# An SSD layer whose chunks are issued in two parts, with one projection task between them

## The chip, the cores and the metric

The kernel runs on one core of one Trainium2 chip. The metric is the device time of one execution in microseconds (us), as a median over runs. "The profile" is one execution recorded by the hardware profiler. TensorE is PE, its weight loads are PEld, VectorE is DVE, ScalarE is ACT, GpSimd is POOL, and SP issues the DMAs.

## What is computed

One streaming step of a two-layer encoder, for 1024 frames of a new stream and 32 frames of a running one, with D_MODEL = 1024. Each layer is a mixer and a SwiGLU feed-forward network, each after an RMS norm and added to the residual.

```python
def ssd_scan(x, dt, A, Bm, Cm, S0):          # layer 0: 32 heads of 64, in 4 groups, state 128
    ...
    def step(S, inp):
        xc, dtc, Bc, Cc = inp
        cum = jnp.cumsum(dtc * Ag, axis=1)
        seg = cum[:, :, None] - cum[:, None, :]
        decay = jnp.where(mask, jnp.exp(jnp.where(mask, seg, 0.0)), 0.0)
        xdt = xc * dtc[..., None]
        cb = jnp.einsum('btgn,bsgn->btsg', Cc, Bc)
        y = jnp.einsum('btsg,btsgh,bsghp->btghp', cb, decay, xdt)
        y = y + jnp.einsum('btgn,bghpn->btghp', Cc, S) * jnp.exp(cum)[..., None]
        ...
        S = jnp.exp(last)[..., None, None] * S + jnp.einsum('bsgh,bsghp,bsgn->bghpn', w_end, xdt, Bc)
        return S, y
def swiglu(h, w_gate, w_up, w_down):         # hidden 2816
    return (jax.nn.silu(h @ w_gate) * (h @ w_up)) @ w_down
```

Layer 1 has an HGRN2 mixer (`gla_scan`, 8 heads of 128) in place of the SSD mixer, and a final norm follows.

## The kernel before

**Halves.** Time is cut into two halves. Half 0 has 512 columns in one block; half 1 has 544 (512 of the prompt and 32 of the sample) in two blocks of 272. The stages follow one another: SSD layer (to about 873 us of the profile), FFN of layer 0 (to about 1600), HGRN layer, FFN of layer 1. Inside the FFN the two halves also follow one another.

**Products.** Every float32 operand of a projection is split into a high and a low part, so a product has three matmuls for each of its k steps: L282 (high by high), L283 (low activations), L284 (low weights). Activations are `h`, `l` (normed input), `yh`, `yl` (SSD output), `fh`, `fl` (FFN hidden); weights come by DMA into `raw`, ACT rounds them into `wh`, and DVE subtracts to get `wl`. FFN gate and up products (`ffn_unit`) combine blocks first, and their matmuls are L917 to L919.

**SSD.** A unit is a half and a group of 8 heads: eight units, u0 to u3 in half 0 and u4 to u7 in half 1. A unit has 4 chunks of 128 frames (5 in half 1). `ssd_chunk` issues for a chunk: C by B (L479), four transposes of x (L484), of which DVE makes `xdt` and `xw`; ACT and DVE make the decays in `cumB` (loaded by a broadcast DMA); the transpose of B (L499), copied by ACT to `Btok`; the state's part (L506); `Btok` by `xw` (L509), which renews the state; and eight matmuls `xdt` by decays for y (L520). After each chunk the loop issues a share of the unit's `tasks`: output projections of the unit before, z projections of this one, convolution projections of the next. After the last chunk comes `ssd_gate`, with a sum over partitions by a matmul (L299). Where half 1 begins, `ssd_dt` computes the steps `dt`, and L402 transposes them for all chunks.

**FFN.** The hidden units are worked in slabs of two; a slab's hidden columns `fh`, `fl` then go through w_down (`ffn_outs`, L282 to L284), added to the residual `acc`. Each gate or up unit loads two weight halves and builds eight split weights, some from sums such as `s1` = a21 + a22 (DVE, shown as `s<-raw`). The last slab's outputs of a half are mixed with the next half's norm.

**Order.** A scheduler writes one order per engine from the program's order, its buffers and priorities; each engine then runs its own row of instructions in that order, and waits at an instruction whose operand or buffer is not there.

Of the kernel before, what the change touches and what calls it, by code (L numbers as in the profile page):

```python
# [16 lines left out]
P = 128  # L17
# [13 lines left out]
NG = 4  # L31
# [10 lines left out]
TW = 552  # L42
BUFS = {"xn": 16, "x": 12, "ys": 8, "cb": 4, "xd": 2, "ec": 1, "ss": 1, "xr": 2, "n": 4, "w": 3, "s": 5}
WIDTH = {k: 512 if k == "xr" else TW if k in ("x", "w") else LEN[1] for k in BUFS}


@with_exitstack
def trunk_kernel(ctx, tc, x_prompt, x_sample, state_ssd, cache_conv, state_hgrn,
# [22 lines left out]

    def small(s, w=P, dt=F32):
        return sp.tile([P, w], dt, tag="s", bufs=BUFS["s"], name=nm(s))

# [40 lines left out]

    ident = cp.tile([P, P], F32, name="ident")
    make_identity(nc, ident)
    ones = cp.tile([P, P], F32, name="ones")
    V.memset(ones, 1.0)
    epsc = cp.tile([P, 1], F32, name="epsc")  # L120
    V.memset(epsc, EPS)
    lss = cp.tile([P, 13], F32, name="lss")
    epst = lss[:, 12:13]
    mhalf = cp.tile([P, 8], F32, name="mhalf")
    G.memset(mhalf, -0.5)
    cmask = cp.tile([P, P], F32, name="cmask")
# [4 lines left out]
    rmask = cp.tile([P, LEN[1]], F32, name="rmask")  # L131
    V.memset(rmask, 1.0)
# [3 lines left out]
    for i in range(2):  # L136
        t = cp.tile([P, P], F32, name=f"scz{i}")
        V.memset(t, 0.0)
        scz.append(t)


    acc = [[cp.tile([P, LEN[h]], F32, name=f"acc{h}_{m}") for m in range(KD)] for h in range(2)]

    xss = cp.tile([P, 2, 9], F32, name="xss")
    xr = cp.tile([P, 9], F32, name="xr")

# [36 lines left out]

    vc = cp.tile([P, NVC], F32, name="vc")
    cw = cp.tile([P, 96], F32, name="cw")
    cc = cp.tile([P, 72], F32, name="cc")
    dtb = cp.tile([P, 1], F32, name="dtb")
    acol = cp.tile([P, 1], F32, name="acol")
    dcol = cp.tile([P, 16], F32, name="dcol")
    lbt = cp.tile([P, 6, 8], F32, name="lbt")  # L190
    c1, c0, nc1 = lbt[:, 3, :], lbt[:, 4, :], lbt[:, 5, :]
# [68 lines left out]
    def wraw(parts, kt):  # L260
        raw = wp.tile([P, 1024], F32, tag="raw", bufs=3, name=nm("raw"))
        r3 = raw.rearrange("p (k c) -> p k c", k=kt)
        for (lo, hi, src) in parts:
            dma(r3[:, :, lo:hi], src.rearrange("(k p) c -> p k c", p=P))
        return raw

    @lifted("wl")
    def wsplit(raw, kt):
        wh = wp.tile([P, 1024], F32R, tag="ws", bufs=6, name=nm("wh"))
        wl = wp.tile([P, 1024], F32R, tag="ws", bufs=6, name=nm("wl"))  # L270
        act(wh, raw, AF.Copy)
        tt(wl, raw, wh.bitcast(F32), SUB)
        return (wh.rearrange("p (k c) -> p k c", k=kt), wl.rearrange("p (k c) -> p k c", k=kt))

    def product(ps, w, col, x, b0, bn):

        wh, wl = w
        n = len(x)
        for k, (xh, xl) in enumerate(x):
            a, b = wh[:, k, col:col + P], wl[:, k, col:col + P]  # L280
            mh, ml = xh[:, b0:b0 + bn], xl[:, b0:b0 + bn]
            PE.matmul(ps[:, :bn], a, mh, start=(k == 0), stop=False)  # L282
            PE.matmul(ps[:, :bn], a, ml, start=False, stop=False)  # L283
            PE.matmul(ps[:, :bn], b, mh, start=False, stop=(k == n - 1))  # L284
# [18 lines left out]

    XN = ["xn"] * 16
    XN2 = ["x"] * 12 + ["cb"] * 4
# [16 lines left out]
    def norm(h, wc, out, tags, blocks=None, r=None):  # L322

        for (b0, bn) in blocks or ((0, LEN[h]),):
# [17 lines left out]

    carry = cp.tile([P, NCT, 3], F32, name="carry")
    newc = cp.tile([P, 2, 3, NCT], F32, name="newc")
    Sst = [cp.tile([P, 512], F32, tag="st", bufs=NG, name=f"Sst{g}") for g in range(NG)]
    cumd = [dp.tile([32, LEN[h]], F32, name=f"cumd{h}") for h in range(2)]
# [4 lines left out]
    def ssd_dt(h, xn, blocks):  # L351
# [33 lines left out]
        act(pk[96:128, :L], cum[96:128, :L], AF.Exp)  # L385
        lastc = cp.tile([P, 5], F32, name=f"lastc{h}")
        V.tensor_copy(lastc[96:128, :4], pk[96:128, P - 1:H1:P])
# [4 lines left out]
        dma(lastd[h][:, :nch], lastc[96:128, :nch])  # L392
        elast = cp.tile([P, 32, 5], F32, tag="elast", bufs=2, name=f"elast{h}")
        dma(elast[:, :, :nch], lastd[h][:, :nch].unsqueeze(0).to_broadcast([P, 32, nch]))
        return pk, None, elast

    def ssd_cols(h):
        pk, _, elast = dts[h]
        cols = cp.tile([P, 5, P], F32, tag="cols", bufs=1, name=f"cols{h}")
        for c, (o, n, _) in enumerate(CHUNKS[h]):  # L400
# [173 lines left out]
    def ssd_layer(after, w0):  # L574
# [16 lines left out]
        for i, (h, g) in enumerate(units):  # L591
# [56 lines left out]

    Shb = [cp.tile([P, 512], F32, tag="st", bufs=NG, name=f"Sh{i}") for i in range(2)]
    Sh = [Shb[e // 4][:, (e % 4) * P:(e % 4 + 1) * P] for e in range(8)]  # L650
# [136 lines left out]
    def hgrn_layer(after):  # L787
# [4 lines left out]
        for i, (h, e) in enumerate(units):  # L792
# [38 lines left out]

    def x_stat(h, tag):

        keep = T(tag, "rkeep")
        return rstd_of([acc[h][m][:, :LEN[h]] for m in range(KD)], BLK[h], 1.0 / D, LEN[h], keep)

    def norm_pieces(h, wc, out, blocks, r):

        def piece(m, b0, bn):
            xf = T("n", "xf")  # L840
            stt(xf[:, :bn], acc[h][m][:, b0:b0 + bn], vc[:, wc + m:wc + m + 1], r[:, b0:b0 + bn], MUL, MUL)
            if m == len(out):
                out.append((T("xn", "h", F32R), T("xn", "l", F32R)))
            xh, xl = out[m]
# [43 lines left out]
    def unit_weights(src):  # L888
# [9 lines left out]

        s1 = T("xr", "s1")[:, :512].rearrange("p (k c) -> p k c", k=4)
        yield hl(a11)  # L900
# [137 lines left out]

    def ffn_outs(layer, h, s, hid):

        ws = {}

        def piece(m, b0, bn):
# [58 lines left out]
    def mixer_ffn(mixer, layer, wc, nxt):  # L1102
# [16 lines left out]
        due = ffn_half(layer, 1, xn[1], tx[1], 1, lambda: r.append(nxt and x_stat(0, "ss")),  # L1119
                       [2] if nxt else [1, 1])  # L1120
# [111 lines left out]
```

## Time and profile before

| | |
|---|---|
| median of 3 runs | 2942.97 us (2942.57 to 2947.24) |
| the profiled execution | 2942.06 us |
| its span, first to last instruction | 2940.3 us |
| PE busy | 2855.9 us, 97% |
| PEld busy | 2618.4 us, 89% |
| DVE busy | 2205.6 us, 75% |
| ACT busy | 1551.3 us, 53% |
| mean granted clock of PE | 0.994 |

The profiled execution's time is 1.8 us longer than its span. Matmuls are pipelined, so the busy shares of PE overlap its waits a little; what an engine waited for is in the views of waits, and one place is read in a timeline.

### The profile page before, as it was taken

The page shows a single profiled execution, that of the slowest core. Times are in us where ns is not written, and L with a number is a line of the kernel's source. Part 1 is how long each engine was busy: PE and PEld are TensorE (multiplying, and loading weights), DVE is VectorE, ACT ScalarE, POOL GpSimd, SP SyncE. Part 2 cuts the span into 40 slices and gives each one's busy share as a digit, 9 for nine tenths or more (in the row PEclk, how much of TensorE's full clock was granted, in tenths as well). Part 3 has the DMA queues.
Part 4 walks back from the last instruction along what each step waited for, and adds up shares of the span by engine and source line. Part 5 has one row for each costly group of instructions (what it writes and reads, how often), then busy time and mean ns, then how long its engine had stood idle before and what let it go on. Part 6 is the DMA issues. An engine that isn't in the chain of part 4 may idle for free.

```text
span 2940.3 us, 49353 instructions
## 1 busy us (share of the span) xinstructions
PE 2855.9 (97%) x19655; PEld 2618.4 (89%) x19655; DVE 2205.6 (75%) x3879; ACT 1551.3 (53%) x2944; POOL 52.7 (2%) x156
## 2 busy tenths in 40 slices
PE   7999999999999999999999999999999999999998
PEld 6777788989988999899999888899988999999997
DVE  6877787877887987897777555655578977887777
ACT  6745545554643654455544555655554644454445
POOL 0000001000100000000000000000000000000000
PEclk9999999999999999999999999999999999999999
DMA  5443424343333333322333222222222333323332
GB/s 146 123 111 94 108 76 122 106 113 98 109 80 105 98 98 108 108 80 87 101 94 99 79 79 80 69 76 76 78 84 87 108 96 99 111 87 94 94 94 103
DMA packets 401346, 283.42 MB, mean 96 GB/s; under 512 B 28873, under 2 KB 386778, under 8 KB 401114
## 3 DMA queue, kind: packets, MB, share of 16 engines
q1 hardware_dynamic: 401114, 280.25, 32.7%
q8 instruction: 154, 2.52, 0.4%
q14 instruction: 78, 0.64, 0.1%
HBM read 272.39 MB, written 7.82 MB: 95 GB/s over the span
## 4 chain that ended last, share of the span: by engine, by line
PE 75%; DVE 12%; DMA 6%; ACT 5%; issue 2%; SPq 0%; DVEq 0%; POOL 0%; ACTq 0%; POOLq 0%
PE mm L282 16%; PE mm L284 16%; PE mm L283 16%; PE mm L919 3%; PE mm L917 3%; PE mm L918 3%; PE sc L919 3%; PE sc L917 3%; PE sc L918 3%; DMA cumB<-cumd 3%; DMA raw<-in_ffn_w_gate_dram 2%; DVE wh L89 2%; ACT wh L86 1%; PE sc L509 1%; ACT cumB L86 1%
## 5 line engine op out<-in xcount | busy, mean ns | idle before, releaser
L86 ACT ACTIVATE wh<-raw 128x512 fp32r<-128x512 f32 (+1 forms) x688 | 554.2, 817 | 592.4 <-PE mm L283 363.3
L282 PE MATMUL mm<-h,wh 128*128 128x272 f32 (+2 forms) x2064 | 675.0, 328 | 7.9 <-ACT h L86 3.9
L284 PE MATMUL mm<-h,wl 128*128 128x272 f32 (+2 forms) x2064 | 668.5, 324 | 2.7 <-DVE wl L89 2.7
L283 PE MATMUL mm<-l,wh 128*128 128x272 f32 (+2 forms) x2064 | 668.3, 324 | 1.3 <-DVE l L89 0.9
L89 DVE TENSOR_TENSOR wl<-raw,wh 128x1024 fp32r<-128x1024 f32 x308 | 376.0, 1222 | 150.7 <-ACT wh L86 149.3
L282 PEld LDWEIGHTS mm<-h,wh 128*128 128x128 f32 x2064 | 390.0, 189 | 38.1 <-ACT h L86 4.9
L284 PEld LDWEIGHTS mm<-h,wl 128*128 128x128 f32 x2064 | 390.2, 189 | 33.0 <-DVE wl L89 3.9
L283 PEld LDWEIGHTS mm<-l,wh 128*128 128x128 f32 x2064 | 390.4, 189 | 30.9 <-DVE l L89 3.1
L282 PE MATMUL mm<-fh,wh 128*128 128x272 f32 (+1 forms) x1056 | 343.2, 326 | 8.9 <-DVE fxd L89 7.8
L283 PE MATMUL mm<-fl,wh 128*128 128x272 f32 (+1 forms) x1056 | 342.2, 325 | 1.8 <-DVE fl L89 1.8
L89 DVE TENSOR_TENSOR acc<-mm,acc 128x272 f32<-128x272 f32 (+1 forms) x512 | 259.6, 524 | 110.3 <-PE mm L284 107.6
L284 PE MATMUL mm<-fh,wl 128*128 128x272 f32 (+1 forms) x1056 | 341.1, 324 | 0.6 <-DVE wl L89 0.6
L89 DVE TENSOR_TENSOR wh<-raw,wh 128x512 fp32r<-128x512 f32 x380 | 258.2, 688 | 20.6 <-ACT wh L86 17.7
L917 PE MATMUL mm<-th,wh 128*128 128x272 f32 (+1 forms) x912 | 260.9, 286 | 0.4 <-ACT s L86 0.4
L919 PE MATMUL mm<-th,wh 128*128 128x272 f32 (+1 forms) x912 | 259.6, 285 | 0.2 <-DVE wh L89 0.2
L918 PE MATMUL mm<-tl,wh 128*128 128x272 f32 (+1 forms) x912 | 259.6, 285 | 0.0
L282 PEld LDWEIGHTS mm<-fh,wh 128*128 128x128 f32 x1056 | 198.8, 189 | 26.9 <-DVE fxd L89 9.3
L283 PEld LDWEIGHTS mm<-fl,wh 128*128 128x128 f32 x1056 | 199.6, 189 | 17.7 <-DVE fl L89 3.4
L284 PEld LDWEIGHTS mm<-fh,wl 128*128 128x128 f32 x1056 | 199.5, 189 | 16.1 <-DVE wl L89 1.0
L917 PE MATMUL sc<-h,wh 128*128 128x272 f32 (+1 forms) x608 | 173.7, 286 | 0.5 <-ACT wh L86 0.5
L917 PEld LDWEIGHTS mm<-th,wh 128*128 128x128 f32 x912 | 171.7, 188 | 2.5 <-ACT s L86 1.7
L919 PE MATMUL sc<-h,wh 128*128 128x272 f32 (+1 forms) x608 | 173.3, 285 | 0.0
(261 smaller groups left out, 5961.0 us busy)
## 6 DMA issues: line engine op xcount, KB each, us to landing
raw<-in_ffn_w_down_dram SPq DMA_DIRECT2D x90, 512.0 KB, 3.5
raw<-in_ffn_w_gate_dram SPq DMA_DIRECT2D x88, 512.0 KB, 4.9
raw<-in_ffn_w_up_dram SPq DMA_DIRECT2D x88, 512.0 KB, 3.8
raw<-in_ssd_in_w_dram SPq DMA_DIRECT2D x80, 512.0 KB, 4.6
raw<-in_hgrn_in_w_dram SPq DMA_DIRECT2D x64, 512.0 KB, 4.1
cumB<-cumd SPq DMA_DIRECT2D x64, 256.0 KB, 4.1
raw<-in_ssd_out_w_dram SPq DMA_DIRECT2D x32, 512.0 KB, 3.7
raw<-in_hgrn_out_w_dram SPq DMA_DIRECT2D x16, 512.0 KB, 3.2
```

The lines of the kernel that those rows point to most:

```text
L86: A.activation(out=out, in_=in_, func=f, **kw)
L89: (eng or V).tensor_tensor(out=out, in0=a, in1=b, op=op)
L282: PE.matmul(ps[:, :bn], a, mh, start=(k == 0), stop=False)
L283: PE.matmul(ps[:, :bn], a, ml, start=False, stop=False)
L284: PE.matmul(ps[:, :bn], b, mh, start=False, stop=(k == n - 1))
L509: PE.matmul(pp, Btok[:n, :], xw[:n, :], start=True, stop=True)
L917: PE.matmul(ps[:, :n], a, mh, start=(k == 0 and not more), stop=False, skip_group_check=True)
L918: PE.matmul(ps[:, :n], a, ml, start=False, stop=False, skip_group_check=True)
L919: PE.matmul(ps[:, :n], b, mh, start=False, stop=(k == 3), skip_group_check=True)
```

## The change

It does six things. `ssd_chunk` ends after `Btok` and returns its second part, `ssd_chunk_b` (L506, L509, the state, L520, y); the loop issues the first part, one task, the second part, then the other tasks. The tile `ec` (the decays for the state's part) gets two buffers. Constants, residual, states and small tiles become slices of one tile `fixed`, the normed input becomes one tile `xn`, and all other tiles take a width of 552 or 2 or 4 times that, so that tags share equal slots of memory; `s1` has two places in the SSD state tiles. `unit_raw` is counted after its use, so gate weights load into `raw` and up weights into `Y`, the other way round than before. `ffn_outs(..., staggered=True)` at three ends of halves runs the first two (half 0) or three (half 1) outputs together: first k = 0, 1 of each, then k = 2, k = 3, and then adds them. And `x_stat` keeps its result in a state tile. No product, and no other arithmetic, is added or left out.

```diff
-BUFS = {"xn": 16, "x": 12, "ys": 8, "cb": 4, "xd": 2, "ec": 1, "ss": 1, "xr": 2, "n": 4, "w": 3, "s": 5}
-WIDTH = {k: 512 if k == "xr" else TW if k in ("x", "w") else LEN[1] for k in BUFS}
+FIXED = 14368
+BUFS = {"x": 12, "ys": 8, "cb": 4, "xd": 2, "ec": 2, "ss": 1, "xr": 2, "n": 4, "w": 3}
+WIDTH = {k: TW for k in BUFS}
...
+    fixed = cp.tile([P, FIXED], F32, name="fixed")
+    used = [0]
+
+    def place(w):
+        used[0] += -(-w // 16) * 16
+        return fixed[:, used[0] - -(-w // 16) * 16:][:, :w]
...
-    def product(ps, w, col, x, b0, bn):
+    def product(ps, w, col, x, b0, bn, ks=None):
 
         wh, wl = w
         n = len(x)
-        for k, (xh, xl) in enumerate(x):
+        for k in ks or range(n):
+            xh, xl = x[k]
             a, b = wh[:, k, col:col + P], wl[:, k, col:col + P]
...
+        return lambda: ssd_chunk_b(h, g, c, S, cums, ec, xdt, xw, Btok, Cx, u)
+
+    @lifted("chunk")
+    def ssd_chunk_b(h, g, c, S, cums, ec, xdt, xw, Btok, Cx, u):
+        o, n, smp = CHUNKS[h][c]
+        cols, elast = dts[h]
+        h0, Y = g * 8, u["Y"]
...
-                ssd_chunk(h, g, c, Ss if smp else Sst[g], loads, u)
+                second = ssd_chunk(h, g, c, Ss if smp else Sst[g], loads, u)
                 loads = nxt
                 q = -(-len(tasks) // (nch - c))
-                for t in tasks[:q]:
+                for t in tasks[:1]:
+                    t()
+                second()
+                for t in tasks[1:q]:
...
     def unit_raw(src):
 
-        NU[0] += 1
         if NU[0] % 2:
-            t = sp.tile([P, 4 * LEN[1]], F32, tag="Y", bufs=1, name=nm("raw2"))
+            t = sp.tile([P, 4 * TW], F32, tag="Y", bufs=1, name=nm("raw2"))
             halves = [t[:, q * 1024:(q + 1) * 1024] for q in range(2)]
         else:
-            halves = [wp.tile([P, 1024], F32, tag="raw", bufs=3, name=nm("raw")) for _ in range(2)]
+            halves = [wp.tile([P, 2 * TW], F32, tag="raw", bufs=3, name=nm("raw"))[:, :1024] for _ in range(2)]
         out = []
...
-        s1 = T("xr", "s1")[:, :512].rearrange("p (k c) -> p k c", k=4)
+        NU[0] += 1
+        s1 = st[NU[0] % 2][:, :512].rearrange("p (k c) -> p k c", k=4)
...
-    def ffn_outs(layer, h, s, hid):
+    def ffn_outs(layer, h, s, hid, staggered=False):
...
-            ps = psum_mm((2, 3, 4))
-            product(ps, ws[c], (m * P) % cols, hid, b0, bn)
+            return ws[c], (m * P) % cols, psum_mm((2, 3, 4))
+
+        def whole(m, b0, bn):
+            w, col, ps = piece(m, b0, bn)
+            product(ps, w, col, hid, b0, bn)
             accumulate(h, m, ps, b0, bn)
-        return [lambda m=m, b=b: piece(m, *b) for m in range(KD) for b in BLK[h]]
+
+        def first(outs):
+
+            ready = [piece(m, *b) for m, b in outs]
+            for ks in ((0, 1), (2,), (3,)):
+                for (w, col, ps), (m, (b0, bn)) in zip(ready, outs):
+                    product(ps, w, col, hid, b0, bn, ks)
+            for (w, col, ps), (m, (b0, bn)) in zip(ready, outs):
+                accumulate(h, m, ps, b0, bn)
+
+        outs = [(m, b) for m in range(KD) for b in BLK[h]]
+        rest = [lambda m=m, b=b: whole(m, *b) for m, b in outs]
+        if staggered:
+            n = 2 if len(BLK[h]) == 1 else 3
+            return [lambda: first(outs[:n])] + rest[n:]
+        return rest
...
-        due = ffn_half(layer, 0, xn[0], tx[0], HEAD, lambda: r.append(x_stat(1, "ec")), [2])
-        run(mixed(ffn_outs(*due[0]), norm_pieces(1, wc, xn[1], BLK[1], r[0])))
+        due = ffn_half(layer, 0, xn[0], tx[0], HEAD, lambda: r.append(x_stat(1, st[2])), [2])
+        run(mixed(ffn_outs(*due[0], staggered=True), norm_pieces(1, wc, xn[1], BLK[1], r[0])))
```

The order on PE at the second chunk of u2 (half 0), before: `sc_2717` holds the transposed x, `sc_2748` the L509 product, `mm_2769` a z projection of eight k steps.

```order
L484 MATMUL sc_2717<-ident,ca_2474 128x128
L499 MATMUL sc_2738<-ident,ca_2259 128x128
L506 MATMUL sc_2742<-ca_2302,Sst_127 128x128 x4
L282 MATMUL mm_2769<-h_226,wh_2764 128x512
L283 MATMUL mm_2769<-l_227,wh_2764 128x512
L284 MATMUL mm_2769<-h_226,wl_2765 128x512
...
L282 MATMUL mm_2769<-h_238,wh_2764 128x512
L283 MATMUL mm_2769<-l_239,wh_2764 128x512
L509 MATMUL sc_2748<-xw_2723,Btok_2740 128x512
L520 MATMUL sc_2752<-cumB_2623,xdt_2722 64x128 x4
```

The same chunk now, where the lines are L509 for the transposes of x, L524 for that of B, L304 to L306 for a product, L538 for the state's part, L541 for `Btok` by `xw`, and `fixed` stands for what was `ident`, `Btok` or the state:

```order
L509 MATMUL sc_2635<-fixed,ca_2395 128x128
L304 MATMUL mm_2666<-xn,wh_2661 128x512
L305 MATMUL mm_2666<-xn,wh_2661 128x512
L524 MATMUL sc_2656<-fixed,ca_2180 128x128
L306 MATMUL mm_2666<-xn,wl_2662 128x512
...
L306 MATMUL mm_2666<-xn,wl_2662 128x512
L538 MATMUL sc_2693<-ca_2223,fixed 128x128 x4
L541 MATMUL sc_2699<-xw_2641,fixed 128x512
L552 MATMUL sc_2703<-cumB_2544,xdt_2640 64x128 x4
```

Between the last transpose of x and the product by `xw` stood 8 projection matmuls; now there are 21. At the same place of half 1 (u4) it was 12, 6 and 12 matmuls of 272 columns in its three middle chunks, and is 35 now.

The order on DVE in half 1 of the FFN of layer 0, where the outputs of a slab begin (near 1334 us), before: `s_2371_14535` is `s1` of a gate unit, `fxd_14491` the tile that is made out of a PSUM bank, `sq` belongs to a norm.

```order
L89 TENSOR_TENSOR fw_14081<-s_2292_13982 128x272
L92 SCALAR_TENSOR_TENSOR fw_14080<-ft_14209,fw_14080 128x544
L89 TENSOR_TENSOR s_2371_14535<-raw_2370_14532 128x512
L89 TENSOR_TENSOR sq_14464<-sq_14464,sq_14466 128x512
L89 TENSOR_TENSOR fxd_14491<-sc_14160,s_2311_14119 128x272
```

The same place now; `fixed<-raw_14315,raw_14316` is `s1`, `fixed<-mm` rows add an output to the residual, `wl` rows split w_down.

```order
L101 TENSOR_TENSOR wl_14064<-raw_14061,wh_14063 128x1024
L104 SCALAR_TENSOR_TENSOR fw_13866<-ft_13993,fw_13866 128x544
L101 TENSOR_TENSOR sq_14247<-sq_14247,sq_14249 128x512
L101 TENSOR_TENSOR fxd_14274<-sc_13944,s_2143_13905 128x272
L101 TENSOR_TENSOR wl_14126<-raw_14123,wh_14125 128x1024
L104 SCALAR_TENSOR_TENSOR fw_13867<-ft_13996,fw_13867 128x544
L101 TENSOR_TENSOR fixed<-mm_14005,fixed 128x272
...
L101 TENSOR_TENSOR fixed<-mm_14033,fixed 128x272
L101 TENSOR_TENSOR sq_14247<-sq_14247,sq_14258 128x512
L101 TENSOR_TENSOR fixed<-raw_14315,raw_14316 128x512
```

`s1` moved from ahead of `fxd` to behind it and behind three additions; a split of w_down weights (`wl_14064`) moved ahead of `fxd`. Three other places where a slab's outputs begin in half 1 (near 1538, 2638 and 2839 us) have the same move.

The order on PE where the steps of half 1 are transposed, before: `mm_4364` is the last of a run of convolution projections.

```order
L282 MATMUL mm_4364<-h_3531,wh_4331 128x272
L283 MATMUL mm_4364<-l_3532,wh_4331 128x272
L284 MATMUL mm_4364<-h_3531,wl_4332 128x272
L402 MATMUL sc_4402<-ident,dt_3841 128x128
L402 MATMUL sc_4405<-ident,dt_3841 128x128
L402 MATMUL sc_4408<-ident,dt_3841 128x128
L282 MATMUL mm_4440<-yh_3950,wh_4436 128x512
```

And now (L427 is the transpose):

```order
L427 MATMUL sc_4283<-fixed,dt_3705 128x128
L427 MATMUL sc_4286<-fixed,dt_3705 128x128
L427 MATMUL sc_4289<-fixed,dt_3705 128x128
L306 MATMUL mm_4076<-xn,wl_4070 128x272
L304 MATMUL mm_4076<-xn,wh_4069 128x272
```

142 matmuls of 272 columns, which stood ahead of these three transposes, now stand behind them and ahead of the last two.

## Rows read from the trace of the kernel before

**Rows 1.** The page's first part: busy time of each engine.

```profile
PE 2855.9 (97%) x19655; PEld 2618.4 (89%) x19655; DVE 2205.6 (75%) x3879; ACT 1551.3 (53%) x2944; POOL 52.7 (2%) x156
```

**Rows 2.** PE's waits: line waited for, us in total, times, longest us.

```profile
PE sc L509 <- DVE xw L89: 8.9, 10, 1.4
PE mm L282 <- DVE fxd L89: 7.8, 7, 2.1
PE sc L509 <- ACT wh L86: 5.5, 4, 1.8
...
PE sc L509 <- ACT Btok L86: 2.3, 1, 2.3
PE sc L402 <- ACT pre L86: 2.1, 1, 2.1
PE mm L283 <- DVE fl L89: 1.8, 3, 0.7
...
PE sc L506 <- ACT Btok L86: 1.1, 1, 1.1
```

**Rows 3.** Timeline of u2's second chunk: start, us, engine, line, idle before.

```profile
282.62 1.28 ACT L86 ACTIVATE cumB<-cumB,cols 128x128 f32<-128x128 f32 x4 [2.91 <-DMA cumB<-cumd]
283.02 0.60 PE L484 MATMUL sc<-ident,ca 128*128 128x128 f32 x4
...
284.38 0.48 PE L282 MATMUL mm<-h,wh 128*128 128x512 f32 x1
...
286.09 0.40 PE L283 MATMUL mm<-l,wh 128*128 128x512 f32 x1
286.22 0.69 DVE L92 SCALAR_TENSOR_TENSOR z<-z,mm 128x512 f32<-128x512 f32 x1 [1.91 <-ACT z L86]
...
287.43 0.68 DVE L89 TENSOR_TENSOR xw<-sc,cols 128x512 f32<-128x512 f32 x1
...
288.25 1.10 PE L509 MATMUL sc<-xw,Btok 128*128 128x512 f32 x2 [1.76 <-ACT wh L86]
```

**Rows 4.** Timeline of u5's second chunk.

```profile
606.64 0.60 PE L484 MATMUL sc<-ident,ca 128*128 128x128 f32 x4
...
609.85 0.68 DVE L89 TENSOR_TENSOR xw<-sc,cols 128x512 f32<-128x512 f32 x1
```

**Rows 5.** Busy time by stretch (chunks of u2, then u3): PE, PEld, DVE, ACT, POOL, clock.

```profile
273.00:313.00 40.00, 35.21 (x214) 26.68 (x213) 24.68 (x39) 17.55 (x42) 0.00 (x0) 1.00 0.39 104
372.00:425.00 53.00, 50.35 (x302) 40.68 (x301) 46.45 (x78) 22.07 (x47) 0.00 (x0) 0.97 0.32 80
```

**Rows 6.** The same view of two short stretches behind waits.

```profile
1337.80:1341.20 3.40, 3.40 (x17) 3.40 (x16) 2.81 (x4) 1.81 (x4) 0.00 (x0) 0.50 0.29 77
406.00:409.40 3.40, 3.40 (x25) 3.06 (x21) 1.89 (x3) 0.89 (x2) 0.00 (x0) 0.50 0.02 5
```

**Rows 7.** Timeline where half 1's steps are made and transposed.

```profile
446.50 0.72 DVE L89 TENSOR_TENSOR dt<-dt,dt 32x544 f32<-32x544 f32 x1
...
461.36 0.25 PEld L402 LDWEIGHTS sc<-ident,dt 128*128 128x128 f32 x2
...
463.92 0.44 PE L402 MATMUL sc<-ident,dt 128*128 128x128 f32 x1 [2.07 <-ACT pre L86]
```

**Rows 8.** Timeline where two slabs' outputs begin, FFN of layer 0, half 1.

```profile
1333.45 0.29 PE L919 MATMUL mm<-th,wh 128*128 128x272 f32 x1
...
1334.20 0.29 PE L919 MATMUL mm<-th,wh 128*128 128x272 f32 x1
1334.89 0.69 DVE L89 TENSOR_TENSOR s<-raw 128x512 f32<-128x512 f32 x1 [2.51 <-DMA raw<-in_ffn_w_gate_dram]
...
1336.59 0.40 PE L282 MATMUL mm<-fh,wh 128*128 128x272 f32 x1 [2.10 <-DVE fxd L89]
...
1540.38 1.06 ACT L86 ACTIVATE wh<-raw 128x1024 fp32r<-128x1024 f32 x1 [4.58 <-DMA raw<-in_ffn_w_down_dram]
```

**Rows 9.** Waits of DVE and ACT for FFN weights, in the same form.

```profile
DVE s L89 <- DMA raw<-in_ffn_w_gate_dram: 32.8, 16, 3.5
```

More of the change, by code (lines that the diff above doesn't have):

```diff
@@ L70, in T, with slot, small @@
         return tp.tile([P, WIDTH[tag]], dt, tag=tag, bufs=BUFS[tag], name=nm(s))
-    def small(s, w=P, dt=F32):
-        return sp.tile([P, w], dt, tag="s", bufs=BUFS["s"], name=nm(s))
+    def slot(tag, s):
+        return T(tag, s, F32R) if isinstance(tag, str) else tag
+    rings = {"diag": (0, 2), "cbm": (2, 2), "Btok": (4, 2), "hT": (0, 2), "hSp": (2, 4), "fss": (4, 2), "nco": (0, 1)}
+    at = {}
+    def small(s, w=P):
+        at[s] = at.get(s, -1) + 1
+        if s == "hec":
+            return hec[at[s] % 3][:, :w]
+        first, n = rings[s]
+        return smalls[first + at[s] % n][:, :w]
     turn = [0]
@@ L113, in trunk_kernel @@
     MUL, ADD, SUB = ALU.mult, ALU.add, ALU.subtract
-    ident = cp.tile([P, P], F32, name="ident")
+    fixed = cp.tile([P, FIXED], F32, name="fixed")
[3 more added lines that the diff above has]
+        return fixed[:, used[0] - -(-w // 16) * 16:][:, :w]
+    smalls, hec = [place(P) for _ in range(6)], [place(16) for _ in range(3)]
+    ident = place(P)
     make_identity(nc, ident)
-    ones = cp.tile([P, P], F32, name="ones")
+    ones = place(P)
     V.memset(ones, 1.0)
-    epsc = cp.tile([P, 1], F32, name="epsc")
+    epsc = place(1)
     V.memset(epsc, EPS)
-    lss = cp.tile([P, 13], F32, name="lss")
+    lss = place(13)
     epst = lss[:, 12:13]
-    mhalf = cp.tile([P, 8], F32, name="mhalf")
+    mhalf = place(8)
     G.memset(mhalf, -0.5)
-    cmask = cp.tile([P, P], F32, name="cmask")
+    cmask = place(P)
     V.memset(cmask, 1.0)
@@ L130, in trunk_kernel @@
     umask = cmask.bitcast(U32)
-    rmask = cp.tile([P, LEN[1]], F32, name="rmask")
+    rmask = place(LEN[1])
     V.memset(rmask, 1.0)
@@ L136, in trunk_kernel @@
     for i in range(2):
-        t = cp.tile([P, P], F32, name=f"scz{i}")
+        t = place(P)
         V.memset(t, 0.0)
         scz.append(t)
-    acc = [[cp.tile([P, LEN[h]], F32, name=f"acc{h}_{m}") for m in range(KD)] for h in range(2)]
-    xss = cp.tile([P, 2, 9], F32, name="xss")
-    xr = cp.tile([P, 9], F32, name="xr")
+    acc = [[place(LEN[h]) for m in range(KD)] for h in range(2)]
+    xss = place(2 * 9).rearrange("p (a b) -> p a b", b=9)
+    xr = place(9)
     def x_rows(h, c):
@@ L182, in over_partitions @@
             PE.matmul(out[:, c * P:c * P + n], ones[:n, :], d[:n, :n], start=True, stop=True)
[L184 to L190, printed above, removed]
+    vc = place(NVC)
+    cw = place(96)
+    cc = place(72)
+    dtb = place(1)
+    acol = place(1)
+    dcol = place(16)
+    lbt = place(6 * 8).rearrange("p (a b) -> p a b", b=8)
     c1, c0, nc1 = lbt[:, 3, :], lbt[:, 4, :], lbt[:, 5, :]
@@ L260, in wraw @@
     def wraw(parts, kt):
-        raw = wp.tile([P, 1024], F32, tag="raw", bufs=3, name=nm("raw"))
+        raw = wp.tile([P, 2 * TW], F32, tag="raw", bufs=3, name=nm("raw"))[:, :1024]
         r3 = raw.rearrange("p (k c) -> p k c", k=kt)
@@ L302, in rstd_of @@
         return r
-    XN = ["xn"] * 16
+    colt = place(5 * P)
+    xnt = cp.tile([P, 16, LEN[1]], F32R, name="xn")
+    XN = [xnt[:, i] for i in range(16)]
     XN2 = ["x"] * 12 + ["cb"] * 4
@@ L340, in accumulate @@
         tt(d, ps[:, :bn], d, ADD)
-    carry = cp.tile([P, NCT, 3], F32, name="carry")
-    newc = cp.tile([P, 2, 3, NCT], F32, name="newc")
-    Sst = [cp.tile([P, 512], F32, tag="st", bufs=NG, name=f"Sst{g}") for g in range(NG)]
+    carry = place(NCT * 3).rearrange("p (a b) -> p a b", b=3)
+    newc = place(2 * 3 * NCT).rearrange("p (a b c) -> p a b c", b=3, c=NCT)
+    st = [place(TW) for _ in range(NG)]
+    Sst = [t[:, :512] for t in st]
     cumd = [dp.tile([32, LEN[h]], F32, name=f"cumd{h}") for h in range(2)]
@@ L385, in ssd_dt @@
         act(pk[96:128, :L], cum[96:128, :L], AF.Exp)
-        lastc = cp.tile([P, 5], F32, name=f"lastc{h}")
+        lastc = place(5)
         V.tensor_copy(lastc[96:128, :4], pk[96:128, P - 1:H1:P])
@@ L392, in ssd_dt @@
         dma(lastd[h][:, :nch], lastc[96:128, :nch])
-        elast = cp.tile([P, 32, 5], F32, tag="elast", bufs=2, name=f"elast{h}")
+        elast = place(160).rearrange("p (h c) -> p h c", c=5)
         dma(elast[:, :, :nch], lastd[h][:, :nch].unsqueeze(0).to_broadcast([P, 32, nch]))
@@ L646, in half_two_dt @@
         dts[1] = ssd_dt(1, xns[1], BLK[1])
-    Shb = [cp.tile([P, 512], F32, tag="st", bufs=NG, name=f"Sh{i}") for i in range(2)]
+    Shb = [t[:, :512] for t in st[:2]]
     Sh = [Shb[e // 4][:, (e % 4) * P:(e % 4 + 1) * P] for e in range(8)]
```

29 lines of the change are left out of this document (14 added, 15 removed).

## Prediction

> **What bounds the kernel now.** I read the page's first lines first: PE is busy for 2855.9 of 2940.3 us, so idle PE time is at most 84.4 us in the coarse count, and DVE follows at 75% [rows 1]. The number and sizes of the matmuls are the same after the change, so it can gain only where PE waits, or where it runs at a lower clock. So the view of PE's waits comes next [rows 2]. The reader is to see there three places that the change touches. The product `Btok` by `xw` (L509) waits for 8.9 + 5.5 + 2.3 = 16.7 us, and the state's part once for 1.1. The first output of an FFN slab (L282) waits 7.8 us for DVE's `fxd`. And two small ones are L402 with 2.1 and `fl` with 1.8. Together that is 29.5 us, one per cent of the time.
>
> Then each place is read in the timeline, to see what the wait hangs on. In a chunk of u2 PE transposes x at 283.02, runs eight projection matmuls, the last at 286.09, and then stands until 288.25, though DVE ends `xw` at 287.43 + 0.68 = 288.11. DVE came to `xw` late: it first waited 1.91 us for a z tile of ACT, and ACT had stood for 2.91 us before a `cumB` that a DMA brings [rows 3]. So the chunk needs 288.25 - 283.02 = 5.2 us from the transposes of x to `xw`, and PE has some 3 us of work to put between. In a chunk of u5 the transposes start at 606.64 and `xw` ends at 609.85 + 0.68 = 610.53, so 3.9 us are needed [rows 4].
>
> Where a slab's outputs begin, PE ends the hidden products at 1334.20 + 0.29 and starts the outputs at 1336.59. Between them DVE's next instruction is `s1` of a coming gate unit, which waits 2.51 us for that unit's weights; `fxd`, which empties the PSUM bank that the output needs, stands behind it [rows 8]. PE idles for a transfer that it doesn't need for a long time yet. [...]
>
> **The change, part by part.**
>
> *Chunks in two parts.* Between the last transpose of x and L509 there are now 21 matmuls of 512 columns in half 0 and 35 of 272 in half 1, for 8 and for 6 or 12. One of 512 takes (286.09 - 284.38) / 7 = 0.24 us from start to start in a run of eight [rows 3], of which the first is a little slow: 0.235. One of 272 takes (1334.20 - 1333.45) / 6 = 0.125 in a run of seven [rows 8]. So the cover is 21 x 0.235 = 4.9 us and 35 x 0.125 = 4.4 us, to which the transposes and the state's part come, 284.38 - 283.02 = 1.3 us [rows 3]: 6.2 against the needed 5.2, and 5.7 against 3.9. The margin is 1 to 1.8 us. The waits at stake are 16.7 + 1.1, less 2.3 (u3, below): 15.5 us. I take -14, since a margin of 1 us may fail at a chunk or two, and u0, which has few tasks, keeps its small share; the ends are -15.5 and -7 (half of the chunks still short). What hides the moved tasks' own work is DVE, 62% busy in such a stretch (24.68 of 40 us) [rows 5]. `ec` with two buffers and more places for `cumB` let the DMAs of rows 3 start a chunk earlier; this goes the same way, and is not counted twice.
>
> [...]
>
> *u3.* In half 0's last unit DVE is busy for 46.45 of 53 us, 88% [rows 5]; half 1's norm is among its tasks. The split changes which chunk has the long task between its parts: one gets more than 10 us of cover, and one is left with about as little as before. The wait of 2.3 and its clock dip of 1.7 go or move. I take -2, with ends -4 and +2.
>
> *Transposes of the steps.* These move ahead of 142 matmuls of 272 columns, 142 x 0.125 = 17.8 us. In the profile they start at 461.36, so they would be reached at 443.6; the last DVE instruction that makes `dt` ends at 446.50 + 0.72 = 447.2 [rows 7]. So PE would stand for about 3.6 us where it now stands 2.1, and what DVE must do before grows a little by the new order: I take +2, ends 0 and +6.
>
> *FFN, gate weights in `raw`, up weights in `Y`.* At the places of the 7.8 us DVE's order has `fxd` ahead of `s1` now, and `s1` behind three additions, which PE reaches 5 us later. The waits go (-7.8), and the dip behind the one at 1334 (-1.7): -9.5. Ahead of `fxd` now stands a split of w_down weights, and behind the waiting `fxd` stands PE. This weight's transfer must be early: at 1538 ACT had to wait 4.58 us for w_down and began only at 1540.38 [rows 8]. In the new order of SP that load stands ahead of the gate's loads, not behind them, and its tile comes free earlier. Ends: -10 and 0.
>
> *Staggered outputs.* Three ends of halves wait 1.8 us for `fl` in all [rows 2]; now the first slab's share of two or three outputs, 12 or 18 matmuls instead of 6, covers the making of `fl`. -1.5, ends -2 and 0.
>
> *The rest* (slices of one tile, `x_stat` in a state tile, the other turns of order) moves no PE work of which I could find a wait: 0, ends -3 and +3.
>
> Sum: -14 - 2 + 2 - 9.5 - 1.5 = -25. The profiled execution took 2942.06 us, 1.8 more than its span; less 25 that is 2917. The median of the runs is 0.9 above the profiled one, so I say 2918.
>
> **The rivals.**
>
> *The FFN waits stay under another name.* DVE's head of queue would be the w_down split in place of `s1`, waiting for a DMA as ACT does at 1540.38 [rows 8]. Then the 9.5 come back: 2918 + 9.5 = 2927. For it: ACT's wait there; against: that load's place ahead of the gate's. [...]
>
> *The chunk waits turn into others.* A unit's DVE and ACT work is not less, and the gate's sum at a unit's end and the next unit's first chunk follow it. If the unit is bound by the chain of its decays rather than by one chunk's cover, half of the 14 comes back, and L402 and u3 at their bad ends cost 8 more: 2918 + 7 + 8 = 2933. For it: u3's 88%; against: 62% in u2.
>
> *Slower.* Gate weights now go through the three buffers of `raw`, which they share with w_down. If w_down's splits hold these tiles, gate loads start late, and `s1` is late for its own split weights in each gate unit. DVE already waits 32.8 us in 16 places for gate weights [rows 9], hidden by PE's outputs. There are 2816 / 256 = 11 gate units in each half of each FFN, 44 in all: 25 / 44 = 0.57 us of PE per unit eats the gain, from 31 / 44 = 0.7 on the time is above 2949, and a loss of 2.1 - 0.7 = 1.4 us in each, what PE lost at 1336.59 beyond `s1` itself [rows 8], would give 2918 + 62 = 2980. I take 2955, which is 0.85 us a unit. Against it: where outputs begin, PE has 16 of 12 matmuls, 24 us, before the next product that could need `s1`.
>
> *Nothing happens.* The scheduler orders by priority, and the split might be undone by it; the order shows that it isn't.
>
> *More.* Freed slots let loads start earlier everywhere, and small waits that I left at 0 go too: 2908.
>
> **How the numbers follow.** The sum 0.60 (own range 2911 to 2924), FFN waits stay 0.13 (2927), chunk waits turn into others 0.12 (2933, a third of it at no change), slower 0.05 (2955), no change 0.03, more 0.07 (2908). Two executions differ measurably from 0.2% on, 5.9 us: faster is below 2937, slower above 2949. That gives faster 0.88, same 0.08, slower 0.04. The range that leaves out less than 2 in 10: 2906 to 2935.
>
> **What would show it.** Right: PE's waits have no L509 row above 3 us, and no L282 row for `fxd`; the timeline where a slab's outputs begin shows `fxd` right after the norm's square; the clock is 1.00 there; L402 waits 3 to 5 us for `dt`. Wrong: L509 or the state's part still wait for `xw` by 5 us or more (cover too short); L282 waits for `wl` or `fxd` (w_down late); L917 to L919 wait for split weights in the gate units (gate late); or PE's waits fall as said and the time doesn't, which would mean that the waits of rows 2 don't measure what PE loses.

## The result and the profile after

The changed kernel took 2914.46 us (median of 4 runs, 2912.04 to 2915.4), against 2945.1 us (4 runs) for the kernel before on the same chip: a ratio of 0.9893, 95% interval 0.9877 to 0.9909. The forecast was 2918, inside 2906 to 2935, so the number held. One of its two large terms, the FFN's, held for its reason. The other did not: what the forecast put down to the split chunk comes from the room for tiles, and in the changed kernel the split itself costs time.

The page of the changed kernel, first lines, which answer to [rows 1]:

```profile
span 2912.9 us, 49100 instructions
## 1 busy us (share of the span) xinstructions
PE 2851.6 (98%) x19655; PEld 2621.6 (90%) x19655; DVE 2203.9 (76%) x3879; ACT 1550.5 (53%) x2946; POOL 56.1 (2%) x156
```

The span is 27.4 us shorter, and PE's busy time only 4.3: what went is idle time of PE. Its waits now (line waited for, us in total, times, longest), against [rows 2]:

```profile
PE sc L427 <- DVE dt L101: 3.8, 1, 3.8
...
PE mm L304 <- ACT pre L98: 3.5, 3, 2.3
...
PE sc L509 <- DVE fixed L101: 2.6, 1, 2.6
...
PE mm L304 <- DVE fxd L101: 0.6, 3, 0.2
...
PE mm L305 <- DVE fl L101: 0.5, 1, 0.5
```

L541, the product that was L509, has no row at all; the 16.7 us are gone. So are the 7.8 us for `fxd` (0.6 left) and most of `fl`. New are a wait for `dt` (L427, the transposes of the steps), one for `pre` in front of a convolution product, and one of the transposes of x (L509 now) for DVE.

Where a slab's outputs begin, the timeline that answers to [rows 8] is now:

```profile
1319.14 0.69 DVE L101 TENSOR_TENSOR sq<-sq,sq 128x512 f32<-128x512 f32 x1
...
1319.75 0.43 DVE L101 TENSOR_TENSOR fxd<-sc,s 128x272 f32<-128x272 f32 x1
...
1320.23 0.19 PEld L304 LDWEIGHTS mm<-fh,wh 128*128 128x128 f32 x1 [0.17 <-DVE fxd L101]
```

`fxd` runs right behind the norm's square, and PE's weight load waits 0.17 us where PE stood 2.10. The granted clock in the 8 us behind it is 1.00; the dip of [rows 6] is gone.

To see where the rest of the time went, the same PE instruction is looked up in two traces. The table gives its start in a kernel minus its start in the kernel before, as the median over the PE instructions of the 8 us ahead of the named moment of the kernel before. "Again" is the changed kernel on another chip, "whole" the first experiment below, "slots" and "cb4" later ones.

```
moment before, us           after   again   whole   cb4    slots
   95  start                 -2.6    -1.9    -4.0   -2.4    -3.0
  372  end of u2            -15.5   -12.4   -18.5   -2.9    -1.1
  425  end of u3's chunks   -18.6   -17.0   -20.0   -3.9    -2.2
  535  u4's chunks done     -17.5   -14.7   -23.9   -4.9    -1.5
  752  u7 begins            -22.9   -20.1   -29.5   -0.7    -1.4
  950  end of the SSD stage -12.2   -11.2   -31.4   -0.7    -1.2
 1320  FFN 0, half 1        -14.2   -14.8   -34.0   -5.0    -2.7
 1360  its outputs          -17.9   -18.5   -37.7   -8.7    -5.3
 1600  end of FFN 0         -19.7   -20.9   -40.2  -11.2    -7.2
 2285  end of HGRN          -21.8   -23.6   -43.9  -14.5    -8.1
 2915  end                  -25.9   -28.6   -51.0  -19.8    -8.8
```

The changed kernel is 20 us and more ahead at 752 us, and gives 9 to 11 back by the end of the SSD stage, in its last unit. What follows gains 14 and 17 us. All columns but the first come from other chips, on which the kernel before takes 2935.5 to 2936.6 us, some 6 us less than in the profile that they are compared with; a part of their gains at the end is that.

### The profile page after: what moved, and what is told of

Its sections match the earlier page's. It is cut to its first block, busy times and chain, and to the rows that moved or that the text cites. A ratio compares the mean times of both kernels' runs of the same rounds, so it can differ in the third digit from the quotient of the medians.

```text
span 2912.9 us, 49100 instructions
## 1 busy us (share of the span) xinstructions
PE 2851.6 (98%) x19655; PEld 2621.6 (90%) x19655; DVE 2203.9 (76%) x3879; ACT 1550.5 (53%) x2946; POOL 56.1 (2%) x156
## 5 line engine op out<-in xcount | busy, mean ns | idle before, releaser
L304 PE MATMUL mm<-xn,wh 128*128 128x272 f32 (+2 forms) x1552 | 526.9, 340 | 5.3 <-ACT pre L98 3.5
L305 PE MATMUL mm<-xn,wh 128*128 128x272 f32 (+2 forms) x1552 | 521.0, 336 | 1.2 <-DVE xn L101 1.2
L306 PE MATMUL mm<-xn,wl 128*128 128x272 f32 (+2 forms) x1552 | 519.1, 335 | 1.7 <-DVE wl L101 1.6
L101 DVE TENSOR_TENSOR fixed<-mm,fixed 128x272 f32<-128x272 f32 (+1 forms) x512 | 262.7, 524 | 186.5 <-PE mm L306 184.8
L304 PE MATMUL mm<-fh,wh 128*128 128x272 f32 (+1 forms) x1056 | 343.5, 326 | 1.7 <-DVE fixed L101 0.9
L306 PE MATMUL mm<-fh,wl 128*128 128x272 f32 (+1 forms) x1056 | 342.4, 325 | 0.0
L304 PEld LDWEIGHTS mm<-xn,wh 128*128 128x128 f32 x1552 | 294.0, 190 | 36.1 <-ACT pre L98 4.2
L306 PEld LDWEIGHTS mm<-xn,wl 128*128 128x128 f32 x1552 | 294.4, 190 | 31.8 <-DVE wl L101 3.3
L305 PEld LDWEIGHTS mm<-xn,wh 128*128 128x128 f32 x1552 | 294.1, 190 | 28.0 <-DVE xn L101 1.7
L304 PEld LDWEIGHTS mm<-fh,wh 128*128 128x128 f32 x1056 | 198.6, 188 | 19.4 <-DVE fxd L101 2.1
L306 PEld LDWEIGHTS mm<-fh,wl 128*128 128x128 f32 x1056 | 198.9, 188 | 15.5
L951 PE MATMUL sc<-xn,wh 128*128 128x272 f32 (+1 forms) x608 | 173.2, 285 | 0.0
L953 PE MATMUL sc<-xn,wh 128*128 128x272 f32 (+1 forms) x608 | 172.9, 284 | 0.0
```

Source lines behind the costliest of these rows:

```text
L101: (eng or V).tensor_tensor(out=out, in0=a, in1=b, op=op)
L951: PE.matmul(ps[:, :n], a, mh, start=(k == 0 and not more), stop=False, skip_group_check=True)
L953: PE.matmul(ps[:, :n], b, mh, start=False, stop=(k == 3), skip_group_check=True)
```

## The experiments

All ratios are to the kernel before, measured on the same chip between the runs; the kernel before took 2945.1 us on the first chip, and 2936.56, 2935.53 and 2936.6 on the three of the experiments, so ratios are compared, not times from different chips. The first four ran on one chip, the second four on another and the last four on a third.

**Whole chunks.** The second part follows the first at once; everything else is as changed.

```diff
-                for t in tasks[:1]:
-                    t()
                 second()
-                for t in tasks[1:q]:
+                for t in tasks[:q]:
                     t()
```

> The changed kernel with its chunks whole again: the second part follows the first at once, then the tasks. Theory (the cover is what pays): L509's wait of before comes back, some 12 to 16 us of PE's waits in the SSD stage, and the time is 2926 to 2930 against 2914 of the changed kernel. Rival (the buffers pay: second ec tile, more places for the decays): the SSD stage keeps its gain, the time is within 4 us of 2914, and L509 waits under 5 us.

2890.02 us, ratio 0.9838 (0.9823 to 0.9852): faster than either theory said. The rival has the reason: the SSD stage keeps its gain without the split. Without the split the kernel is faster by 0.55% of the time before, some 16 us. L541 waits little, though only its old few matmuls cover it, and ACT hardly waits for `cumB`. In the kernel before ACT waited for `cumB` and w_down like this:

```profile
ACT wh L86 <- DMA raw<-in_ffn_w_down_dram: 149.6, 41, 5.0
...
ACT cumB L86 <- DMA cumB<-cumd: 75.4, 35, 6.2
```

and with whole chunks and all the rest of the change (the third row is PE's):

```profile
ACT wh L98 <- DMA raw<-in_ffn_w_down_dram: 10.0, 8, 1.6
...
ACT cumB L98 <- DMA cumB<-cumd: 5.4, 10, 0.9
...
PE sc L541 <- DVE xw L101: 1.6, 2, 1.0
```

**The split alone.** The kernel before, with `ssd_chunk` cut behind `Btok` and the loop of the change; one `ec`, old tiles.

```diff
-                ssd_chunk(h, g, c, Ss if smp else Sst[g], loads, u)
+                second = ssd_chunk(h, g, c, Ss if smp else Sst[g], loads, u)
...
+                for t in tasks[:1]:
+                    t()
+                second()
+                for t in tasks[1:q]:
```

> The kernel before with the chunk's split alone; one ec buffer, old tiles. Theory (cover): most of the 16.7 us of L509 goes, less what u3, u7 and the transposes of the steps give back: 2930 to 2935 against 2943 to 2945. Rival (buffers): with one ec buffer and the old slots nothing is gained, 2941 to 2947, or it is slower, since the second part keeps ec longer.

2936.21 against 2936.56 us, 0.9997 (0.9988 to 1.0006): nothing gained, as the rival said. ACT's wait for `cumB` is still there:

```profile
ACT cumB L86 <- DMA cumB<-cumd: 89.5, 32, 8.7
```

Yet the cover does what the theory says of it: the product by `xw` (L516 here) has 0.8 us of its 16.7 left. Other waits stand in their place. These are PE's between 95 and 873 us (L282 is a projection, L499 the transpose of B, L513 the state's part):

```profile
PE mm L282 <- ACT wh L86: 4.8, 1, 4.8
PE sc L402 <- DVE dt L89: 3.7, 1, 3.7
PE mm L282 <- ACT pre L86: 3.6, 2, 2.3
PE sc L499 <- DVE Y L89: 3.6, 1, 3.6
...
PE sc L516 <- ACT Btok L86: 0.5, 1, 0.5
PE sc L513 <- DVE acc L89: 0.5, 1, 0.5
PE sc L516 <- DVE xw L89: 0.3, 1, 0.3
```

All rows of this view add up to 26.8 us, and to 27.2 in the kernel before. By the table's method the split alone is 5.3 us ahead at 752 us and 3.5 behind at 950, so the last unit takes back what the others gain.

**The swap alone, and the change without the swap.** The counter moves behind `unit_raw` in the kernel before, and back ahead of it in the changed kernel.

```diff
     def unit_raw(src):
 
-        NU[0] += 1
...
+        NU[0] += 1
         s1 = T("xr", "s1")[:, :512].rearrange("p (k c) -> p k c", k=4)
```

> The kernel before with the swap of raw and Y alone (gate into raw, up into Y). Theory: the 7.8 us of fxd and one dip go, 2933 to 2936. Rival (the swap alone only trades the wait for one of late gate weights, the slots or s1's second place are needed too): 2940 to 2950, with PE waiting at L917 to L919 or still at L282.

2928.34 us, 0.9973 (0.9961 to 0.9985). By the table's method the four places give -3.7, -2.1, -2.5 and -1.8 us, together -10.1; by the ratio the whole kernel gains 8 us. This is the forecast's mechanism, without slots or staggering.

> The changed kernel with gate weights loaded into Y and up weights into raw, as before. Theory: the waits of the first output of a slab for fxd come back, 8 us and one clock dip, the FFN stages lose 8 to 11 us: 2922 to 2926. Rival (the freed slots and the staggered outputs moved fxd, not the swap): within 3 us of 2914.

2924.43 us, 0.9951 (0.9934 to 0.9968): 0.58% above the changed kernel, some 17 us, and so more than either theory said. The four places give -5.2 us in place of -9.9; the SSD stage, whose order on PE is the same in both kernels, ended 2 us ahead of before, not 12. So the swap does something at another place as well; the last runs come back to it.

**The changed kernel again**, as a measure beside the next three.

> The changed kernel once more, on the chip of the three runs beside it, as their measure: ratio 0.987 to 0.991 to the kernel before, and an SSD stage with the waits that its profile showed (transposes of the steps 3.8 us, transposes of x in the last unit 2.6).

2906.66 us, 0.9899 (0.9882 to 0.9915), with the same waits.

**Whole chunks in u3 and u7 only.**

```diff
+                last = i in (3, 7)
+                if not last:
+                    for t in tasks[:1]:
+                        t()
                 second()
-                for t in tasks[1:q]:
+                for t in tasks[0 if last else 1:q]:
```

> The changed kernel with whole chunks in the last unit of each half (u3 and u7) and split ones in the others. Theory now (the split is neutral where DVE has room, and costs where a norm stands between the two parts): 12 to 20 us faster than the changed kernel, within 6 us of the kernel with whole chunks (ratio 0.9838 to before). Rival (each split costs a little): half or less of the difference comes back, ratio 0.987 or more.

2897.87 us, 0.9866 (0.9852 to 0.9881): 8.8 us back of the 16 to 18, less than the theory's 12 and just about the rival's half. So the other units' splits cost as well: ACT waits 23.2 us for `cumB` here, and 5.4 with all chunks whole; and PE still waits 3.5 us for `pre` in front of u7's convolutions, a wait that the kernel with whole chunks doesn't have.

**The norm behind the second part.** Split chunks, but in u3 and u7 an output projection comes first in the list and the norm second, so that the projection stands between the first chunk's parts.

```diff
-                    tasks = zs + [half_two_norm] + outs + [half_two_dt]
+                    tasks = zs + outs[:1] + [half_two_norm] + outs[1:] + [half_two_dt]
...
-                tasks = zs + after[:1] + outs + after[1:]
+                tasks = zs + outs[:1] + after[:1] + outs[1:] + after[1:]
```

> The changed kernel with the order of two tasks turned in u3 and u7: an output projection stands between the first chunk's parts, and the norm behind the second part. Theory (the norm between the parts costs): the wait of 2.6 us and its clock dips in u7 go, 5 to 12 us faster than the changed kernel. Rival (the split itself costs there, whatever stands between): within 3 us of it.

2898.01 us, 0.9871 (0.9852 to 0.9889): 8.7 us faster than the changed kernel. The time is the theory's, but the reason holds only in part. What the norm does in the changed kernel is in the timeline of the changed kernel (the run "again"), in u7:

```profile
800.35 1.07 PE L541 MATMUL sc<-xw,fixed 128*128 128x512 f32 x2
...
808.55 1.89 DVE L101 TENSOR_TENSOR xn<-xf,xn 128x512 fp32r<-128x512 f32 x3
810.36 1.40 DVE L104 SCALAR_TENSOR_TENSOR xf<-fixed,rstd 128x512 f32<-128x512 f32 x2
811.68 0.68 DVE L101 TENSOR_TENSOR fixed<-fixed,sc 128x512 f32<-128x512 f32 x1
...
812.41 1.12 PE L509 MATMUL sc<-fixed,ca 128*128 128x128 f32 x4 [2.62 <-DVE fixed L101]
```

The product by `xw` starts at 800.35, but the addition to the state that empties its bank (`fixed<-fixed,sc`) stands on DVE behind the norm's `xf` and `xn`, until 811.68. The next chunk's transposes of x wait 2.62 us for that bank. Then the clock falls; the same place in the profile of the first chip:

```profile
811.30:818.10 6.80, 6.11 (x26) 5.54 (x27) 6.37 (x14) 4.55 (x11) 0.00 (x0) 0.50 0.01 2
```

The granted clock (third number from the end) is 0.50 for 6.8 us. In that stretch 20 projection matmuls take 4.7 us, from 813.39 to 818.09; right behind it they start 0.127 us apart, which makes 2.5 for 20, so by this estimate some 2.2 us more are lost.

With the norm second the wait of 2.62 us is gone, but u7 has another. Now the norm stands on DVE ahead of the next chunk's `xw`, and the product waits for that:

```profile
806.67 1.88 DVE L101 TENSOR_TENSOR xn<-xf,xn 128x512 fp32r<-128x512 f32 x3
808.48 1.40 DVE L104 SCALAR_TENSOR_TENSOR xf<-fixed,rstd 128x512 f32<-128x512 f32 x2
...
811.61 0.67 DVE L101 TENSOR_TENSOR xw<-sc,fixed 128x512 f32<-128x512 f32 x1
...
812.34 1.36 PE L541 MATMUL sc<-xw,fixed 128*128 128x512 f32 x2 [3.96 <-DVE xw L101]
```

From 95 to 860 us the mean granted clock is 0.99, as in the changed kernel. By the table's method only 1.8 us of the gain lie in u7's chunks (800 to 950 us). The changed kernel's waits of 3.8 us for `dt` (L427) and of 3.5 us for `pre` are not in this profile, and a wait of 4.1 us before a sum over partitions (L321) in u3 is new. The edit turns two lists at once, and no run parts u3 from u7.

**One `ec`.** Whole chunks, `"ec": 1`.

> Whole chunks and one ec buffer; the slots of equal size stay. If the slots are what pays (more places for cumB, raw and split weights): within 3 us of whole chunks with two (ratio 0.983 to 0.985). If the second ec pays: L541 and ec wait again, 5 to 15 us more, ratio 0.986 or more.

2891.5 us, 0.9843 (0.9828 to 0.9857): within the interval of two. Here the second `ec` buys nothing measurable; the freed slots remain.

**`cumB` in four fixed places.** Whole chunks; one tile of 4 x 552 for the SSD stage, from which the `cumB` pieces are cut in turn.

```diff
-            cb = T("cb", "cumB")[:, :512].rearrange("p (h t) -> p h t", t=P)
+            cbn[0] += 1
+            cb = cbr[0][:, (cbn[0] % 4) * TW:][:, :512].rearrange("p (h t) -> p h t", t=P)
```

> Whole chunks, all else as changed, but cumB in four fixed places, as many as before. Theory (cumB's places are what the slots give): ACT waits 50 us or more for cumB again, L541 waits 8 to 16 us, and the time is 10 to 20 us above whole chunks with free slots (ratio 0.989 to 0.991 to before). Rival (other tiles' places, raw and split weights, pay): within 4 us of it, ratio 0.983 to 0.985.

2918.81 us, 0.9942 (0.9927 to 0.9957), 1.04% or some 30 us above whole chunks with free places; the table's column "cb4" loses all of the SSD stage's gain, and nothing else. That is the theory's reason, and more than the 10 to 20 us that it priced. The waits (L544 is `Btok` by `xw`, `cbr` is `cumB`, SPq is the queue that issues the DMAs):

```profile
ACT cbr L98 <- DMA cbr<-cumd: 103.8, 43, 9.2
...
PE sc L544 <- DVE xw L101: 10.1, 11, 1.9
...
PE sc L544 <- ACT wh L98: 5.0, 4, 1.4
...
SPq L110 <- DVE cbr L101: 150.2, 32, 13.9
```

This is the kernel before once more: 15.1 us at the product in these two rows, and a DMA queue that stands 150 us until DVE has read old decays. In the kernel before that last row was

```profile
SPq L98 <- DVE cumB L89: 141.4, 32, 13.4
```

and in the kernel with whole chunks it is

```profile
SPq L110 <- DVE cumB L101: 3.9, 1, 3.9
```

**The slots alone.** The kernel before with equal slots and the fixed tile, and none of the rest: whole chunks, one `ec`, gate weights in Y, no staggering. (As a diff to the changed kernel: the first edit above, `"ec": 1`, the swap undone, `if staggered` set to `if False`.)

> The kernel before with the equal slots alone (one fixed tile, widths of 552 and its multiples, s1 in state tiles): whole chunks, one ec, gate weights in Y, no staggered outputs. Theory (the slots pay in the SSD stage): ACT's waits for cumB fall from 75 us to under 10, SSD gains 22 to 30 us, the FFN keeps its fxd waits: ratio 0.987 to 0.990. Rival (the slots need the swap or the second ec to pay): ratio 0.994 or more.

2928.32 us, 0.9974 (0.9965 to 0.9983). The theory fails, and the rival is right: the slots alone give almost nothing in the SSD stage. ACT still waits:

```profile
ACT wh L98 <- DMA raw<-in_ffn_w_down_dram: 157.1, 46, 6.4
...
ACT cumB L98 <- DMA cumB<-cumd: 91.1, 38, 6.4
```

What they do give lies in the FFN, where the theory expected the waits for `fxd` to stay: 1.6 us are left of 7.8, and the four places gain 7.4 us. `s1` still stands ahead of `fxd` there, so this is not the forecast's reason; what it is was not tested.

**Whole chunks without the swap.** Slots and two `ec`, gate weights in Y.

> Whole chunks, all else as changed, but gate weights in Y and up weights in raw, as before. Theory (the swap pays by fxd's order alone): 7 to 11 us slower than with the swap, all of it at the four places where a slab's outputs begin: ratio 0.986 to 0.988. Rival (the swap does more, as the 17 us between the changed kernel and its version without the swap may say): 14 us or more.

2916.43 us, 0.9932 (0.9913 to 0.995): 0.94%, some 27 us above the same kernel with the swap, so the rival. At the end of the SSD stage it is 11.9 us ahead of before, with the swap 31.4; the rest of the difference is in the FFNs. Its waits:

```profile
ACT wh L98 <- DMA raw<-in_ffn_w_down_dram: 155.6, 43, 5.8
...
ACT cumB L98 <- DMA cumB<-cumd: 46.7, 21, 5.3
...
SPq L110 <- DMA raw<-in_ffn_w_down_dram: 160.5, 45, 5.3
...
SPq L110 <- DVE cumB L101: 48.4, 14, 13.9
```

The places that the compiled programs give to tiles, counted as different addresses, go with this. `cumB` has 4 in the kernel before and with the swap alone, 13 with the slots alone, 22 with whole chunks without the swap, 28 with it; `raw` and `Y` together have 4 in every kernel with gate weights in Y and with the swap alone, and 8 in those with slots and the swap. With the waits for `cumB` of the kernel before, the slots alone and whole chunks without and with the swap, 75.4, 91.1, 46.7 and 5.4 us, more places go with shorter waits from 22 on, and 13 don't help. Between the slots alone and this kernel stand only the second `ec` and the staggering, 0.42%; which of the two brings the places was not run.

The waits for w_down are not what holds `cumB` back. ACT's waits for w_down all lie behind 873 us, in the FFNs. And the swap alone, with the 4 places of `raw` and `Y` as before, nearly ends them, while those for `cumB` stay:

```profile
ACT cumB L86 <- DMA cumB<-cumd: 85.9, 39, 8.0
...
ACT wh L86 <- DMA raw<-in_ffn_w_down_dram: 9.7, 9, 1.8
...
SPq L98 <- DVE cumB L89: 140.5, 32, 13.4
```

**No staggered outputs.** Whole chunks, `if staggered` set to `if False`.

> Whole chunks, all else as changed, but no staggered outputs. Theory: the waits for fl at three ends of halves come back, 1 to 3 us; ratio 0.984 to 0.985. Rival (staggering pays nothing): same time and the same stage times at those ends.

2890.34 us, 0.9846 (0.983 to 0.9861): no difference that can be measured. At two of the ends (1210 to 1240, 2500 to 2540 us of before) the gains are 1.1 and 1.3 us with staggering, 0.7 and 1.0 without; at the third there is none.

## Why the forecast was right, and where it was not

*Chunks in two parts, -14.* The size of the stage is within the ends: from 95 us to the end of the SSD stage the changed kernel gains 9.6 and 9.2 us in its two profiles, for -14 with u3's -2 and the +2 of the transposes. The cover itself, 6.2 us against the needed 5.2, held: the split alone leaves 0.8 us of the product's wait. The step that failed is to count the waits that it covers, "15.5 us", as time won. With the split alone PE's waits in the stage add up to 26.8 us in place of 27.2, the time stays (0.03%), and taking the split out of the changed kernel wins 16 us; that is the rival "the chunk waits turn into others". The needed 5.2 us were also taken as a given of the chunk. But [rows 3] themselves show what they consist of: ACT stood 2.91 us for `cumB`, z came late by that, and `xw` behind z. Where `cumB` is there in time the product waits 1.6 us in all with the old cover. The forecast names more places for `cumB`, but as going the same way, and did not count them; in the runs the product waits 15.1 us when `cumB` has 4 places and 1.6 when it has 28.

*u3 and the transposes, -2 and +2.* From 372 to 425 us u3 gains 3.1 and 4.7 us. The transposes wait 3.8 us for `dt`, where 3.6 were said; with the dip behind them (granted clock 0.51 from 432.3 to 435.7 us), the kernel gives 1.1 and 2.3 back between 425 and 535 us. Both held.

*Not in the sum.* From 752 to 950 us the changed kernel loses 10.7 and 8.9 us. It is the rival "the chunk waits turn into others", at two places of the last unit. One is the norm between the parts of u7's first chunk. I had seen such a norm in u3 and priced it there, and overlooked the same list in u7. From 800 to 950 us the changed kernel loses 4.4 us in its second profile and the one with the norm second 2.6, while whole chunks in u3 and u7 gain 1.6; so it is the split there that costs, with a norm close behind it or between its parts. The other place is the wait of 3.5 us for `pre` in front of u7's convolutions, before 800 us. It stays with whole chunks in u3 and u7 and goes when all are whole, but it is not there with the norm second either. What makes it, and what makes the splits of the other units lengthen ACT's wait for `cumB`, was not tested.

*FFN, -9.5.* The four places gain 3.7, 2.1, 2.4 and 1.7 us in the changed kernel, -9.9 together, and -10.1 by the swap alone. The order on DVE, the w_down split ahead of `fxd`, the vanished dip (1.00 where the kernel before has 0.50): all as said. No run shows the 1.7 us that the sum takes for that dip and the part on u3 for another: in the kernel before 15 matmuls start 0.227 us apart from 1337.83 to 1341.23 us, where 0.125 is the distance ahead of the wait, so the dip lasts 3.4 us and costs some 1.5. The swap is enough for this gain, but not the only way to it: the slots alone give 7.4 us at the same places, and in the changed kernel taking the swap out costs 4.7 of the 9.9. What the forecast missed is the swap's second effect: together with the slots it gains some 20 us in the SSD stage of the kernels with whole chunks, where alone it gains 1. There `cumB` has 22 places without it and 28 with it, and the DMA queue's wait for old decays falls from 48.4 to 3.9 us. That the places are the way in which the swap reaches the SSD stage fits the run with four fixed places, but no run has 28 places without the swap.

*Staggering, -1.5.* The waits for `fl` went from 1.8 to 0.5 us, but not by the staggering: without it they are 0.4, and with the swap alone 0.7. The table's method gives 0.7 us for it: mis-sized, within noise.

*The rest, 0.* The start gave 2 to 2.6 and HGRN 2 to 3 us, not foreseen and not tested. A loss of 2.5 us at 2330 us in the first profile is absent in the second.

So the sum came out near because errors cancelled: room for tiles gave more than was counted, and the split took some 16 us of it back. The fastest kernel run here is the changed one with whole chunks, 0.9838.

## What to carry to other kernels

Before covering a wait with more work, follow it back past the engine that is named: here PE waited for DVE (8.9 us at the product), DVE for ACT (1.91 us in u2's second chunk), ACT for a DMA (75.4 us for `cumB`), and the DMA queue for a buffer (141.4 us), and only the last had a remedy that held; covering the first moved the wait. A change of several edits whose sum comes out right has not been explained; run the whole without each part, because two edits may only pay together (slots -8, swap -8, both with staggering and a second `ec` -47 us) and another may cost. And when an instruction group is cut in two, look at what the work between the parts puts on the engine that must release its banks and make its operands: here a norm between them made PE wait 2.62 us for a bank, and one behind the second part 3.96 us for an operand.

## What was not expected of the hardware

Two profiles of the very same kernel on two chips differ by 3.1 us at 372 us, and from 201.2 to 204.6 us the granted clock is 0.50 in the second and 1.00 in the first. The kernel before had medians of 2945.1 and 2935.5 to 2936.6 us on different chips, 0.3%. So stage times of single profiles are taken here as good to some 3 us, and times from different chips are compared as ratios.
